# Latent attention: one batch of value matmuls per head, row maxima placed around it, outputs sent by SyncE, w_o's loads reordered

## The chip, the cores and the metric

The kernel runs on one core of a Trainium2 chip, as one launch. The metric is device time in microseconds. A core has TensorE (PE for its matmuls, PEld for its weight loads), VectorE (DVE), ScalarE (ACT), GpSimd (POOL) and SyncE (SP, which only issues transfers here). ACT can issue transfers too; in the profile these rows are called ACTq, those of SP SPq.

## What is computed

Two layers of a decoder over 1024 positions, width 1024, all in float32. Layer 0 is a latent attention with 12 heads, layer 1 a sliding-window attention; each has cross-attention heads on a memory and is followed by an MLP. The change touches the causal attention of layer 0 alone:

```python
def causal_dense_attention(q, k, v):
    b, s, h, dk = q.shape                  # 1, 1024, 12, 96
    nb = s // Q_BLOCK                      # blocks of 128
    scale = dk ** -0.5
    ...
        sc = jnp.einsum('bqhd,bkhd->bhqk', q_blk, k,
                        preferred_element_type=jnp.float32) * scale
        mask = k_idx[None, :] <= t_idx[:, None]
        sc = jnp.where(mask[None, None], sc, NEG)
        p = jax.nn.softmax(sc, axis=-1).astype(v.dtype)
        return jnp.einsum('bhqk,bkhd->bqhd', p, v)
...
    x = x + jnp.concatenate([mix, cross], axis=-1) @ w_o[i]
```

## The kernel before, in words

**Blocks.** A head's scores are computed transposed, keys on the partitions. A block (G, k) has 128 keys (k from 0 to 7) against the 512 queries of half G, from the diagonal on; twelve blocks cover the causal triangle. `scores` (tile pss) makes a block with three matmuls over 97 rows: high part by high part, and the two mixed products of high and low part. Rows 0 to 63 are the plain part of the key, 64 to 95 the rotary part, and row 96 carries the negated row maximum of each query, so that the exponential needs no bias. On diagonal blocks a mask is added, by a fourth matmul in heads 0, 1, 9, 10 and 11 (`mask_by_pe`), by DVE in the others (L1096). ACT takes the exponential into a tile p (L1098), and POOL adds the p of a half up into acc (L1112). Score tiles, pso, psd, psxt and the small psx come from six psum buffers (`ps1`).

**Row maxima.** `row_max(h, i)` makes the scores of query block i of head h from the high parts alone (psx_i, L909, 128 queries by (i+1)*128 keys), and DVE reduces them to a column of m8 (L911, two instructions, the second reads the result out). Those of i above 3 use one psum tile of two banks with a single buffer (`psx`), so psx_7, psx_6, psx_5 and psx_4 follow one another through it. `max_row(h)` transposes m8 (psxt, L890); ACT copies it to mh (L895) and sends it to row 96 of qh by a transfer on its own queue (L896). The table `WHEN` says at which slot of the stream each row maximum of head h stands, counted from the first slot of head h-1; (8, 7) is `max_row`.

**Values.** `values` multiplies p by v (tile pso, L1064, weights of 64 columns) for a batch of blocks. The list `cuts` sets where batches begin: two per head, after six blocks each. `evac(h)` copies pso to `on` (L1143) and sends it out by two transfers (L1145, L1146); `sums(h)` multiplies acc by ones (psd, weights of 32 columns), copies to sm (L1160) and sends it to den (L1163).

**The division.** For groups of heads (0 to 5, 6 to 9, 10) `rc_split` takes reciprocals of den (L1193), sends them to memory (rcd, L1194), `rc_mul` brings them back spread over 64 partitions (rb, L1186, two buffers) and DVE multiplies the outputs by them (L1206). Head 11 is divided apart.

**w_o.** `wq.step()` takes one step of the list load 0, load 1, split 0, load 2, split 1, load 3, split 2, nothing, split 3: a load is 512 KB by SP (wor, L809, two buffers), a split is one ACT and one DVE instruction (woq, L99 and L100).

**Order.** The loop over n, one step per block, writes everything in one stream; `queued()` holds PE to the order written, and `tc.issue_after` places a step behind a named instruction. Where other engines and queues have freedom, the scheduler sets their order when the program is built. Each engine and each queue then takes its instructions strictly in that order.

Of the kernel before, what the change touches and what calls it, by code (L numbers as in the profile page):

```python
# [9 lines left out]
F32 = mybir.dt.float32  # L10
# [9 lines left out]
P = 128  # L20
D = 1024
S = 1024
NT = S // P
KT = D // P
FF = 4096
H = 12
# [29 lines left out]
def trunk(  # L56
# [7 lines left out]
    nc = tc.nc  # L64
    x = x[0]
    out = out[0]
# [26 lines left out]
    def f32(ap):  # L93
        return ap.bitcast(F32)
# [602 lines left out]
    halves = [slice(0, 512), slice(512, 1024)]  # L697
# [176 lines left out]
    def head_tiles(h, lo):  # L874
        r, e = slice((h % 2) * 64, (h % 2) * 64 + 64), slice((h % 4) * 32, (h % 4) * 32 + 32)
        r_, e_ = slice(h * 64, h * 64 + 64), slice(h * 32, h * 32 + 32)
        qh, ql, kh, kl = bufs_[h % 3]
        for t, n, rope in ((kl, kn_d[r_, :], krl_d), (ql, qn_d[r_, :], qr_d[e_, :])) if lo else ((kh, kn[h // 2][r, :], krh_d), (qh, qn[h // 2][r, :], qr[h // 4][e, :])):
            nc.sync.dma_start(out=f32(t[0:64]), in_=n)
            if h < 3 or t is qh or t is ql:  # L880
                nc.sync.dma_start(out=f32(t[64:96]), in_=rope)
        if h in (1, 2) and lo:
            head_ones(h)
# [57 lines left out]
    for e in range(2):  # L941
        c = slice(e * 512, e * 512 + 512)
# [95 lines left out]
    at = pool("at", "right")  # L1038
# [18 lines left out]
    probs, po_, sp_, acc_, first_p, masked, last_mm = {}, {}, {}, {}, {}, [], []  # L1057
# [34 lines left out]
    def probabilities(h, G, k, ps):  # L1092

        c0 = col0(G, k)
        if k >= 4 * G and not mask_by_pe(h, G, k):
            nc.vector.tensor_tensor(ps[:, 0:P], ps[:, 0:P], dmaskT, ALU.add)  # L1096
        p = at.tile([P, 512], F32, tag="p", bufs=14, name=f"p{h}_{G}_{k}")
        masked[0:1] = [nc.scalar.activation(p[:, c0:], ps, AF.Exp, scale=SC).ins]  # L1098
        probs[(h, G, k)] = p
        if (h, "acc") not in acc_:  # L1100
            acc_[(h, "acc")] = at.tile([P, 1024], F32, tag="acc", bufs=2, name=f"acc{h}")
        a = acc_[(h, "acc")][:, G * 512 : G * 512 + 512]
        if (h, G) not in first_p:
            first_p[(h, G)] = p
            return
        q = first_p[(h, G)]
        if q is not None:
            first_p[(h, G)] = None
            if c0:
                nc.scalar.activation(a[:, :c0], q[:, :c0], AF.Copy)  # L1110
        eng = nc.vector if h == H - 1 and G and k in (1, 2, 3, 7) else nc.gpsimd
        eng.tensor_tensor(a[:, c0:], p[:, c0:], (a if q is None else q)[:, c0:], ALU.add)  # L1112
# [25 lines left out]
    def evac(h):  # L1138

        po, _ = po_.pop(h)  # L1140
        r = slice((h % 2) * 64, (h % 2) * 64 + 64)
        on = at.tile([P, 512], F32, tag="on", bufs=2, name=f"on{h}")
        nc.scalar.activation(on, po, AF.Copy)  # L1143
        dst = qn[h // 2][r, :]
        nc.scalar.dma_start(out=dst.rearrange("p (a c) -> p a c", c=256)[:, 0:4:3, :], in_=on[0:64].rearrange("p (a c) -> p a c", c=256))  # L1145
        nc.scalar.dma_start(out=dst[:, 256:768], in_=on[64:128])  # L1146

    def sums(h, G=None):

        acc = acc_[(h, "acc")]  # L1150
        sp = ps1(f"psd{h}_{G}")
        if G is not None:
            sp_[G] = sp
            for g, a, b in quarters(G):
                product(sp[g * 64 : g * 64 + 64, 0:256], ones, acc[:, G * 512 + a : G * 512 + b], start=True, stop=True)
            return
        for i in range(4):
            product(sp[i * 32 : i * 32 + 32, 0:256], ones[:, 0:32], acc[:, i * 256 : i * 256 + 256], start=True, stop=True)
        sm = at.tile([97, 256], F32, tag="sm", bufs=2, name=f"sm{h}")
        nc.scalar.activation(sm, sp[0:97, 0:256], AF.Copy)  # L1160
        c = [c for c in range(3) if h >= GRP[c]][-1]
        d0 = (h - GRP[c]) * NT
        nc.scalar.dma_start(out=den[c][d0 : d0 + NT, :], in_=sm[0:97:32, :])  # L1163

    def last_o(G, tmp, js=range(2)):

# [11 lines left out]
    den = [at.tile([(b - a) * NT, P], F32, name=f"den{a}") for a, b in zip(GRP, GRP[1:])]  # L1178
    rc_d = [dram.tile([b - a, S], F32, name=f"rcd{a}") for a, b in zip(GRP, GRP[1:])]
    r_tiles = {}  # L1180

    def rc_pair(c, j, i):

        rb = at.tile([P, 512], F32, tag="rb", bufs=2, name=f"rb{c}_{j}_{i}")
        for e in range(min(2, GRP[c + 1] - GRP[c] - 2 * j)):
            nc.sync.dma_start(out=rb[e * 64 : e * 64 + 64, :], in_=rc_d[c][2 * j + e, halves[i]].partition_broadcast(64))  # L1186
        return rb

    def rc_split(c):
# [7 lines left out]
    def rc_mul(c):  # L1197
# [15 lines left out]
    NB = len(blocks)  # L1213
    seq = [(h,) + b for h in range(H) for b in blocks_of(h)]

    WHEN = {
        1: ((4, 0), (3, 1), (2, 2), (1, 3), (0, 4), (8, 7)),
        2: ((7, -4), (6, -1), (5, 1), (4, 2), (3, 3), (2, 3), (1, 4), (0, 5), (8, 7)),
        3: ((7, -5), (6, -4), (5, -1), (4, 1), (3, 1), (2, 2), (1, 3), (0, 4), (8, 7)),
    }  # L1220
    ahead = {}
    for h in range(1, H):
# [1 line left out]
            ahead.setdefault((h - 1) * NB + d, []).append((h, i))  # L1224
    muls = iter(())
    waiting = []
    cuts = [*range(0, (H - 1) * NB, 6), *range((H - 1) * NB, len(seq) + 1, 4)]
    batches = {b + 1: (a, b) for a, b in zip(cuts, cuts[1:])}
    for n in range(len(seq) + 2):
        if n < len(seq):  # L1230
            waiting.append(seq[n])
            if n == len(seq) - 1 or seq[n][2] - 4 * seq[n][1] < 3 or seq[n + 1][2] - 4 * seq[n + 1][1] >= 0:
                scores(*waiting[::-1])
                waiting.clear()
        for g, i in ahead.get(n, ()):
            with queued():
                last_mm[0:1] = [row_max(g, i) if i < NT else max_row(g)[-1]]
        if n in batches:
            values(seq[slice(*batches[n])])
            h, j = divmod(n, NB)  # L1240
            if j == 1 and h < H:
                evac(h - 1)
            if h and j == (7 if h < H - 1 else 5):
                sums(h - 1)
            if n == len(seq) - 3:
                sums(H - 1, 1)
                last_o(1, at.tile([P, 256], F32, tag="on", bufs=2, name="rq1"))
        h, j = divmod(n, NB)
        if n < len(seq):
            if j < 2 and h + 2 < H:  # L1250
                head_tiles(h + 2, j)
        if n % 3 == 1 or n > 11 * NB:
            next(muls, None)
        if n >= 9 * NB and n % 3 == 0:
            with tc.issue_after(masked[0]):
                wq.step()
        for c, (a, b) in enumerate(((9 * NB, 9 * NB + 4), (11 * NB + 1, 11 * NB + 4), (11 * NB + 9, 11 * NB + 10))):
            if n == a:
                rc_split(c)
            if n == b:  # L1260
                muls = rc_mul(c)
# [1115 lines left out]
```

## Time and profile before

| | us |
|---|---|
| runs of the kernel (median, lowest to highest) | 2067.89 (2067.59 to 2069.08) |
| the profiled execution | 2066.95 |
| its span, first to last instruction | 2065.2 |
| PE busy | 2048.0 |
| DVE, ACT, POOL busy | 1420.1, 1070.1, 249.4 |
| the twelve heads | about 232 to 410 of the span |

The span leaves 1.75 us around it. PE is called busy from a matmul's start to its modelled end, so small losses between matmuls show as starts that lie further apart, not as idle time; PEld's idle time before a weight load tells what held a matmul up.

### The profile page before, as it was taken

What the parts mean: (1) busy time and instruction counts of PE and PEld (TensorE: products, weight loads), DVE (VectorE), ACT (ScalarE), POOL (GpSimd) and SP (SyncE); (2) the same over time, 40 slices, a digit from 0 to 9 for tenths busy, and PEclk for the clock granted to TensorE, in tenths of its full rate; (3) what the DMA queues carried; (4) which work ended last, traced back from release to release, by engine and by line L of the source; (5) the groups of instructions that cost most, each with busy time, mean ns of one, the idle gap of its engine ahead of it and who ended that gap; (6) DMA issues with size and microseconds to landing.
All of it is one profiled execution on the core that took longest, in us unless ns stands there. A gap on an engine that the chain in (4) does not pass through costs nothing.

```text
span 2065.2 us, 29537 instructions
## 1 busy us (share of the span) xinstructions
PE 2048.0 (99%) x10035; PEld 1677.5 (81%) x10035; DVE 1420.1 (69%) x2817; ACT 1070.1 (52%) x2335; POOL 249.4 (12%) x357
## 2 busy tenths in 40 slices
PE   9999999999999999999999999999999999999998
PEld 7888877688888888888888888778888888888887
DVE  8767556558877777956566625767977777976565
ACT  7564344557545544444445525866744554444453
POOL 1002366500000000000010134510000000000000
PEclk9999999999999999999999999999999999999999
DMA  6213655442544548835442644442444456944442
GB/s 235 90 39 110 189 124 122 134 150 83 178 137 159 163 155 285 293 97 173 137 129 87 148 105 135 109 148 73 162 154 136 160 163 236 327 130 154 122 123 87
DMA packets 190492, 306.83 MB, mean 149 GB/s; under 512 B 18496, under 2 KB 75013, under 8 KB 190341
## 3 DMA queue, kind: packets, MB, share of 16 engines
q1 hardware_dynamic: 182080, 286.20, 44.2%
q0 software_dynamic: 4144, 13.14, 1.8%
q10 hardware_dynamic: 4116, 5.61, 1.0%
q8 instruction: 79, 1.29, 0.3%
q14 instruction: 73, 0.59, 0.1%
HBM read 194.48 MB, written 89.57 MB: 138 GB/s over the span
## 4 chain that ended last, share of the span: by engine, by line
PE 96%; DVE 2%; DMA 1%; ACT 1%; issue 0%; SPq 0%; ACTq 0%; DVEq 0%
PE psu L1612 6%; PE psu L1613 6%; PE psu L1611 6%; PE psy L1949 6%; PE psy L1951 6%; PE psy L1950 6%; PE psz L1949 4%; PE psz L1951 4%; PE psz L1950 4%; PE psv L1612 4%; PE psv L1613 4%; PE psv L1611 4%; PE pss L1064 3%; PE pswo L111 3%; PE pswo L109 3%; PE pswo L110 3%
## 5 line engine op out<-in xcount | busy, mean ns | idle before, releaser
L99 ACT ACTIVATE g<-i 128x512 fp32r<-128x512 f32 x79 | 49.9, 631 | 105.1 <-PE psy L1950 51.0
L1949 PE MATMUL psy<-g 128*128 128x512 f32 x256 | 100.0, 391 | 0.0
L1950 PE MATMUL psy<-g 128*128 128x512 f32 x256 | 99.7, 389 | 0.0
L1951 PE MATMUL psy<-g 128*128 128x512 f32 x256 | 99.7, 389 | 0.0
L911 DVE CUSTOM_DVE_ANT_0 psx<-psx,wide 128x1024 f32<-128x1024 f32 (+7 forms) x96 | 72.7, 766 | 29.1 <-PE psx L909 28.3
L1098 ACT ACTIVATE p<-pss 128x512 f32<-128x512 f32 (+2 forms) x144 | 64.8, 490 | 49.1 <-DVE pss L1096 20.4
L100 DVE TENSOR_TENSOR g<-i,g 128x512 fp32r<-128x512 f32 x79 | 55.5, 703 | 49.5 <-ACT g L99 49.4
L1112 POOL TENSOR_TENSOR acc<-p,acc 128x512 f32<-128x512 f32 (+2 forms) x92 | 86.1, 942 | 13.3 <-ACT p L1098 9.4
L99 ACT ACTIVATE uh<-i 128x512 fp32r<-128x512 f32 x66 | 41.6, 631 | 85.0 <-PE psz L1950 38.8
L99 ACT ACTIVATE i<-mr 128x512 fp32r<-128x512 f32 x78 | 47.8, 628 | 72.4 <-PE psy L1950 23.5
L100 DVE TENSOR_TENSOR uh<-i,uh 128x512 fp32r<-128x512 f32 x66 | 45.5, 690 | 46.6 <-ACT uh L99 46.6
L1949 PE MATMUL psz<-g 128*128 128x512 f32 x192 | 74.7, 389 | 0.0
L1950 PE MATMUL psz<-g 128*128 128x512 f32 x192 | 74.7, 389 | 0.0
L1951 PE MATMUL psz<-g 128*128 128x512 f32 x192 | 74.7, 389 | 0.0
L1510 ACT ACTIVATE mr<-mr,gcol 128x256 f32<-128x256 f32 (+1 forms) x160 | 63.9, 476 | 12.6 <-DMA mr<-in_mlp_w_up_dram 12.6
L100 DVE TENSOR_TENSOR i<-mr,i 128x512 fp32r<-128x512 f32 x78 | 53.5, 687 | 22.8 <-ACT i L99 22.6
L2069 POOL TENSOR_TENSOR wsr<-wsr,gcol 128x1024 f32<-128x1024 f32 x12 | 23.1, 1925 | 343.3 <-ACT i L99 275.0
L1831 DVE TENSOR_TENSOR mqq<-mqf,mqq 128x512 f32<-128x512 f32 x64 | 43.1, 686 | 23.5 <-DMA mqf<-in_mlp_w_down_dram 23.5
L1951 PEld LDWEIGHTS psy<-g 128*128 128x128 f32 x256 | 48.1, 188 | 10.1
L1950 PEld LDWEIGHTS psy<-g 128*128 128x128 f32 x256 | 48.1, 188 | 9.8
L1949 PEld LDWEIGHTS psy<-g 128*128 128x128 f32 x256 | 48.1, 188 | 9.8
L1064 PE MATMUL pso<-p,v 128*64 128x256 f32 (+1 forms) x480 | 53.8, 367 | 0.0
(659 smaller groups left out, 6746.3 us busy)
## 6 DMA issues: line engine op xcount, KB each, us to landing
i<-hd SPq DMA_DIRECT2D x154, 256.0 KB
hd<-uh SPq DMA_DIRECT2D x76, 256.0 KB
hd<-ul SPq DMA_DIRECT2D x76, 256.0 KB
mr<-in_mlp_w_up_dram SPq DMA_DIRECT2D x36, 512.0 KB
hd<-x SPq DMA_DIRECT2D x72, 256.0 KB
mr<-hd SPq DMA_DIRECT2D x70, 256.0 KB
d<-in_mlp_w_up_dram SPq DMA_DIRECT2D x32, 512.0 KB
mqf<-in_mlp_w_down_dram SPq DMA_DIRECT2D x32, 512.0 KB
```

The lines of the kernel that those rows point to most:

```text
L99: a = nc.scalar.activation(hi, src, AF.Copy)
L100: d = nc.vector.tensor_tensor(lo, src, f32(hi), ALU.subtract)
L911: nc.vector.tensor_tensor_reduce(ps[:, :n], ps[:, :n], wide[h > 1][:, S - n :], -1.0, 3.0e38, ALU.add, ALU.min, accum_out=m)
L1064: last_mm[0:1] = [nc.tensor.matmul(*args, skip_group_check=True, **kw).ins]
L1098: masked[0:1] = [nc.scalar.activation(p[:, c0:], ps, AF.Exp, scale=SC).ins]
L1112: eng.tensor_tensor(a[:, c0:], p[:, c0:], (a if q is None else q)[:, c0:], ALU.add)
L1611: nc.tensor.matmul(ps, wh[:, k, :], xh[:, k, :], start=p in (1, 2, 5) and k == 0, stop=False, skip_group_check=True)
L1612: nc.tensor.matmul(ps, wh[:, k, :], xl[:, k, :], start=False, stop=False, skip_group_check=True)
L1613: nc.tensor.matmul(ps, wl[:, k, :], xh[:, k, :], start=False, stop=k == 3, skip_group_check=True)
L1949: nc.tensor.matmul(ps, ah[:, j, :], bh, start=start, stop=False, skip_group_check=True)
L1950: nc.tensor.matmul(ps, ah[:, j, :], bl, start=False, stop=False, skip_group_check=True)
L1951: nc.tensor.matmul(ps, al[:, j, :], bh, start=False, stop=k == NP - 1, skip_group_check=True)
```

## The change

1. `cuts`: head 0 keeps two batches of six blocks; the twelve blocks of each of heads 1 to 10 form one batch, at slot 1 of the next head; head 11 stays as it was.
2. `sums(h-1)` stands at slot 1 of head h for every head, right behind the batch and `evac`, where it stood at slot 7 (5 in the last head).
3. The tile p has 16 buffers instead of 14.
4. The three output transfers of a head (two of `on`, one of den) are issued by SP, not by ACT.
5. `WHEN`: psx_7 now stands before the blocks (1, 2) and (0, 3), `max_row` behind them; some others are a slot later or earlier.
6. Both halves of `head_tiles(h + 2)` are issued at slot 0 (before at slots 0 and 1).
7. w_o's steps: every second slot from n = 116 (before every third from 108), and also behind the last rb transfer written so far (`last_rb`).

```diff
--- before.py
+++ after.py
@@ -1094,7 +1094,7 @@
         c0 = col0(G, k)
         if k >= 4 * G and not mask_by_pe(h, G, k):
             nc.vector.tensor_tensor(ps[:, 0:P], ps[:, 0:P], dmaskT, ALU.add)
-        p = at.tile([P, 512], F32, tag="p", bufs=14, name=f"p{h}_{G}_{k}")
+        p = at.tile([P, 512], F32, tag="p", bufs=16, name=f"p{h}_{G}_{k}")
         masked[0:1] = [nc.scalar.activation(p[:, c0:], ps, AF.Exp, scale=SC).ins]
         probs[(h, G, k)] = p
         if (h, "acc") not in acc_:
@@ -1142,8 +1142,8 @@
         on = at.tile([P, 512], F32, tag="on", bufs=2, name=f"on{h}")
         nc.scalar.activation(on, po, AF.Copy)
         dst = qn[h // 2][r, :]
-        nc.scalar.dma_start(out=dst.rearrange("p (a c) -> p a c", c=256)[:, 0:4:3, :], in_=on[0:64].rearrange("p (a c) -> p a c", c=256))
-        nc.scalar.dma_start(out=dst[:, 256:768], in_=on[64:128])
+        nc.sync.dma_start(out=dst.rearrange("p (a c) -> p a c", c=256)[:, 0:4:3, :], in_=on[0:64].rearrange("p (a c) -> p a c", c=256))
+        nc.sync.dma_start(out=dst[:, 256:768], in_=on[64:128])
 
     def sums(h, G=None):
 
@@ -1160,7 +1160,7 @@
         nc.scalar.activation(sm, sp[0:97, 0:256], AF.Copy)
         c = [c for c in range(3) if h >= GRP[c]][-1]
         d0 = (h - GRP[c]) * NT
-        nc.scalar.dma_start(out=den[c][d0 : d0 + NT, :], in_=sm[0:97:32, :])
+        nc.sync.dma_start(out=den[c][d0 : d0 + NT, :], in_=sm[0:97:32, :])
 
     def last_o(G, tmp, js=range(2)):
 
@@ -1179,11 +1179,13 @@
     rc_d = [dram.tile([b - a, S], F32, name=f"rcd{a}") for a, b in zip(GRP, GRP[1:])]
     r_tiles = {}
 
+    last_rb = []
+
     def rc_pair(c, j, i):
 
         rb = at.tile([P, 512], F32, tag="rb", bufs=2, name=f"rb{c}_{j}_{i}")
         for e in range(min(2, GRP[c + 1] - GRP[c] - 2 * j)):
-            nc.sync.dma_start(out=rb[e * 64 : e * 64 + 64, :], in_=rc_d[c][2 * j + e, halves[i]].partition_broadcast(64))
+            last_rb[0:1] = [nc.sync.dma_start(out=rb[e * 64 : e * 64 + 64, :], in_=rc_d[c][2 * j + e, halves[i]].partition_broadcast(64)).ins]
         return rb
 
     def rc_split(c):
@@ -1215,8 +1217,8 @@
 
     WHEN = {
         1: ((4, 0), (3, 1), (2, 2), (1, 3), (0, 4), (8, 7)),
-        2: ((7, -4), (6, -1), (5, 1), (4, 2), (3, 3), (2, 3), (1, 4), (0, 5), (8, 7)),
-        3: ((7, -5), (6, -4), (5, -1), (4, 1), (3, 1), (2, 2), (1, 3), (0, 4), (8, 7)),
+        2: ((7, -4), (6, -1), (5, 0), (4, 1), (3, 1), (2, 3), (1, 4), (0, 5), (8, 7)),
+        3: ((7, -6), (6, -4), (5, -1), (4, 1), (3, 1), (2, 3), (1, 4), (0, 5), (8, 7)),
     }
     ahead = {}
     for h in range(1, H):
@@ -1224,7 +1226,7 @@
             ahead.setdefault((h - 1) * NB + d, []).append((h, i))
     muls = iter(())
     waiting = []
-    cuts = [*range(0, (H - 1) * NB, 6), *range((H - 1) * NB, len(seq) + 1, 4)]
+    cuts = [0, 6, *range(NB, (H - 1) * NB, NB), *range((H - 1) * NB, len(seq) + 1, 4)]
     batches = {b + 1: (a, b) for a, b in zip(cuts, cuts[1:])}
     for n in range(len(seq) + 2):
         if n < len(seq):
@@ -1240,19 +1242,20 @@
             h, j = divmod(n, NB)
             if j == 1 and h < H:
                 evac(h - 1)
-            if h and j == (7 if h < H - 1 else 5):
+            if 0 < h < H and j == 1:
                 sums(h - 1)
             if n == len(seq) - 3:
                 sums(H - 1, 1)
                 last_o(1, at.tile([P, 256], F32, tag="on", bufs=2, name="rq1"))
         h, j = divmod(n, NB)
         if n < len(seq):
-            if j < 2 and h + 2 < H:
-                head_tiles(h + 2, j)
+            if j == 0 and h + 2 < H:
+                head_tiles(h + 2, 0)
+                head_tiles(h + 2, 1)
         if n % 3 == 1 or n > 11 * NB:
             next(muls, None)
-        if n >= 9 * NB and n % 3 == 0:
-            with tc.issue_after(masked[0]):
+        if n > 9 * NB + 7 and n % 2 == 0:
+            with tc.issue_after(masked[0]), tc.issue_after(last_rb[0]):
                 wq.step()
         for c, (a, b) in enumerate(((9 * NB, 9 * NB + 4), (11 * NB + 1, 11 * NB + 4), (11 * NB + 9, 11 * NB + 10))):
             if n == a:
```

Three places show the order. The first is PE at the end of head 4 (psx6 are the row maxima of head 6, psxt5 the transposed maxima of head 5); before:

```order
L1064 MATMUL pss4_1_2_3300<-ckh_549,ckl_550 128x512 x2
L1064 MATMUL pss4_0_3_3303<-ckh_549,ckl_550 128x128 x2
L1064 MATMUL pss4_1_2_3300<-ckh_549,ckl_550 128x512
L1064 MATMUL pss4_0_3_3303<-ckh_549,ckl_550 128x128
L890 MATMUL psxt5_3315<-ident_63,m8_5_3155 8x128
L909 MATMUL psx6_7_3321<-kh0_2218,qh0_2216 128x512 x2
L1064 MATMUL pso4_1_3325<-p4_1_0_3224,v_1462 64x256 x2
...
L1064 MATMUL pso4_1_3325<-p4_1_5_3287,v_1462 64x128
L1064 MATMUL psd3_None_3338<-acc3_3061,ones_2563 32x256 x4
L1064 MATMUL pss4_0_2_3346<-ckh_549,ckl_550 128x256 x3
L909 MATMUL psx6_6_3354<-kh0_2218,qh0_2216 128x512
L909 MATMUL psx6_6_3354<-kh0_2218,qh0_2216 128x384
```

and now:

```order
L909 MATMUL psx6_7_3309<-kh0_2218,qh0_2216 128x512 x2
L1064 MATMUL pss4_1_2_3313<-ckh_549,ckl_550 128x512 x2
L1064 MATMUL pss4_0_3_3316<-ckh_549,ckl_550 128x128 x2
L1064 MATMUL pss4_1_2_3313<-ckh_549,ckl_550 128x512
L1064 MATMUL pss4_0_3_3316<-ckh_549,ckl_550 128x128
L890 MATMUL psxt5_3328<-ident_63,m8_5_3143 8x128
L1064 MATMUL pss4_0_2_3333<-ckh_549,ckl_550 128x256 x3
L909 MATMUL psx6_6_3341<-kh0_2218,qh0_2216 128x512
L909 MATMUL psx6_6_3341<-kh0_2218,qh0_2216 128x384
```

The batch and the sums between psx6_7 and psx6_6 are gone; psx6_7 has moved ahead of (1, 2) and (0, 3), so that these, psxt5 and (0, 2) are all that lies between psx6_7 and psx6_6.

The second is PE at the start of head 5, where the whole batch of head 4 now stands, cut after its first rows:

```order
L909 MATMUL psx6_4_3392<-kh0_2218,qh0_2216 128x320 x2
L909 MATMUL psx6_3_3396<-kh0_2218,qh0_2216 128x512
L1064 MATMUL pso4_1_3399<-p4_1_0_3211,v_1462 64x256 x2
L1064 MATMUL pso4_1_3399<-p4_0_0_3225,v_1462 64x256 x2
L1064 MATMUL pso4_1_3399<-p4_1_4_3272,v_1462 64x256 x2
```

It goes on to the blocks up to (1, 7) and (0, 3), 20 instructions in all (16 of 256 columns, 4 of 128), and then the four matmuls of psd4. Before, psd of a head stood six blocks after its last values.

The third is SP in head 9; before:

```order
L1186 DMA rb0_2_1_4308<-rcd0_2572 64x512
...
L881 DMA ql2_2555<-qrd_1944 32x1024
L809 DMA wor0_0_1_4112<-in_w_o_dram 128x2x512
L809 DMA wor0_0_2_4207<-in_w_o_dram 128x2x512
L1186 DMA rb0_2_1_4308<-rcd0_2572 64x512
L1186 DMA rb0_2_0_4363<-rcd0_2572 64x512 x2
L809 DMA wor0_0_3_4294<-in_w_o_dram 128x2x512
```

and now:

```order
L1145 DMA fa1_100<-on8_4083 64x2x256
L1146 DMA fa1_100<-on8_4083 64x512
L1163 DMA den6_2570<-sm8_4092 8x1x128
L809 DMA wor0_0_1_4193<-in_w_o_dram 128x2x512
L1188 DMA rb0_2_1_4309<-rcd0_2572 64x512 x2
L1188 DMA rb0_2_0_4347<-rcd0_2572 64x512 x2
L809 DMA wor0_0_2_4283<-in_w_o_dram 128x2x512
```

The load wor0_0_2, which reuses the buffer of wor0_0_0 and so waits for its split, stood ahead of the second half of rb0_2_1; it now stands behind all four halves, and wor0_0_1 stands between den of head 8 and rb0_2_1.

## Rows read from the trace of the kernel before

**Rows 1.** The page, part 1: busy time and its share of the span.
```profile
PE 2048.0 (99%) x10035; PEld 1677.5 (81%) x10035; DVE 1420.1 (69%) x2817; ACT 1070.1 (52%) x2335; POOL 249.4 (12%) x357
```

**Rows 2.** Windows from one head's first score to the next (heads 4, 7, 8, 10): us, busy (instructions) by engine, clock.
```profile
288.03:302.13 14.10, 14.10 (x100) 10.49 (x98) 8.18 (x25) 6.66 (x17) 9.39 (x10) 1.00 0.50 112
...
330.35:345.05 14.70, 14.38 (x99) 10.49 (x98) 8.96 (x26) 6.66 (x17) 9.38 (x10) 1.00 0.58 147
345.05:359.96 14.91, 14.46 (x99) 10.48 (x98) 10.50 (x29) 6.72 (x17) 10.22 (x10) 1.00 0.63 145
...
374.91:392.94 18.03, 15.46 (x102) 11.46 (x100) 7.92 (x16) 8.27 (x18) 9.90 (x10) 0.91 0.28 82
```

**Rows 3.** Timeline of head 4, PE and PEld: start, us, operation, count, idle before and releaser.
```profile
290.04 1.73 PE L1064 MATMUL pso<-p,v 128*64 128x256 f32 x16
...
291.70 0.96 PE L1064 MATMUL pss<-ckh,ckl 97*128 97x512 f32 x3
...
292.50 0.34 PE L909 MATMUL psx<-kh,qh 96*128 96x384 f32 x1
...
295.63 0.27 PE L890 MATMUL psxt<-ident,m 128*8 128x128 f32 x1
...
295.66 0.71 PE L909 MATMUL psx<-kh,qh 96*128 96x512 f32 x2
...
296.30 2.60 PE L1064 MATMUL pso<-p,v 128*64 128x256 f32 x24
...
298.82 0.64 PE L1064 MATMUL psd_None<-acc,ones 128*32 128x256 f32 x8
...
299.39 0.62 PE L1064 MATMUL pss<-ckh,ckl 97*128 97x256 f32 x3
...
301.67 0.30 PEld L909 LDWEIGHTS psx<-kh,qh 96*128 96x128 f32 x2 [0.17 <-DVE m L911]
...
302.13 0.40 PE L1064 MATMUL pss<-qh,kh 97*128 97x512 f32 x1
...
302.36 0.40 PE L1064 MATMUL pss<-ql,kh 97*128 97x512 f32 x1
```

**Rows 4.** The same stretch, DVE's read-out of psx_7 and ACT's issue of mh.
```profile
296.40 1.23 DVE L911 CUSTOM_DVE_ANT_0 psx<-psx,wide 128x1024 f32<-128x1024 f32 x1 [0.28 <-PE psx L909]
...
296.54 0.71 ACTq L896 DMA_DIRECT2D qh<-mh  x1
...
297.55 0.14 DVE L911 DVE_READ_ACCUMULATOR2_ANT m<- 128x1 f32 x1
```

**Rows 5.** Timeline of head 10, DVE and PE around the multiplications by rb.
```profile
374.17 0.14 DVE L911 DVE_READ_ACCUMULATOR2_ANT m<- 128x1 f32 x1
...
376.13 0.45 PE L1064 MATMUL pss<-ckh,ckl 97*128 97x512 f32 x1
...
376.51 1.65 DVE L1206 TENSOR_TENSOR qn<-rb,qn 128x512 f32<-128x512 f32 x2 [2.20 <-DMA rb<-rcd]
...
379.15 0.80 PE L909 MATMUL psx<-kh,qh 96*128 96x320 f32 x3 [2.57 <-DVE m L911]
...
379.88 2.49 PE L1064 MATMUL pso<-p,v 128*64 128x256 f32 x16
...
383.96 0.41 PE L909 MATMUL psx<-kh,qh 96*128 96x384 f32 x1
```

**Rows 6.** The chain that ends last in 360 to 412 us: start, us, what.
```profile
368.95 2.03 DVE woq L100
371.00 0.39 SPq L809
...
371.43 4.99 DMA rb<-rcd
...
391.44 1.70 DMA den<-sm
...
396.04 3.04 DMA rb<-rcd
```

## What the change does to the time, forecast blind

> **What bounds the kernel now.** I read the page's first part: TensorE is busy 2048.0 of 2065.2 us [rows 1]. So whatever is gained must come out of TensorE's own instruction stream or out of the few places where it waits. The change stays inside the twelve heads of layer 0, so the table of windows came next, one window per head [rows 2]. A steady head takes 14.10 us with PE busy for all 14.10, DVE 8.18, ACT 6.66 and POOL 9.39: four engines of which only PE is full. Heads 7 and 8 take 14.70 and 14.91, and head 10 takes 18.03 with 15.46 busy at a mean granted clock of 0.91. Third, the timeline of one steady head [rows 3, 4], to see where PE's stream is thinner than its matmuls need; fourth, the timeline of head 10 [rows 5]; last, the chain that ends the stretch around it [rows 6]. The profiled execution took 2066.95 us, 0.94 below the median of the runs, 2067.89; I make the sum against 2066.95 and put the 0.94 back at the end. A measurement of this kernel tells about 0.2%, 4.1 us, from no change.
>
> **Part 1, one batch of values for two.** In a head, PE goes from scores to values and back twice. The 16 records at 290.04 last until the scores at 291.70, 1.66 us; the 24 at 296.30 last until the sums at 298.82, 2.52 us [rows 3]. Of the 24, four have 128 columns, of the 16 also four; counting those as half, 22 units take 2.52 and 14 take 1.66: 0.1075 per unit and 0.155 that does not depend on the size. After the batch three score matmuls of 512 columns take 0.80 (291.70 to 292.50) where a matmul takes 0.23 (302.13 to 302.36), so 0.11 is lost there. Ahead of the batch the row-max pair that starts at 295.66 needs 0.64 to the first value matmul, the same sort of pair at 301.67 only 0.46 to 302.13; part of the 0.18 belongs to the transposition just before, so I take 0.10, near the loss on the way out. Together 0.36 us for one way in and out. Ten heads lose one such pair: **-3.6** (bounds -3.1, with no loss on the way in, and -4.4, with 0.18). The sums keep their place behind a batch and their price; the moved evacuation follows the batch as before.
>
> **Part 2, the row maxima.** psx_7 and psx_6 share one psum tile, so psx_6 waits until DVE has read psx_7. Before, the batch of values lay between them and hid it. psx_7 starts at 295.66 and DVE's read-out of it ends at 297.55 + 0.14 [rows 3, 4]: 2.03 us. Now PE has in that time the pair itself (0.46), three matmuls of 512 columns (0.69), three of 128 and the transposition (about 0.12 each, 0.48), three of 256 (0.35): 1.98. It comes 0.05 too early, and a weight load that could not run ahead costs 0.17, as the idle time of PEld before psx_5 shows at 301.67. About 0.24 us in each of the seven heads whose diagonal is masked by DVE (2 to 8); in heads 9 and 10 the mask is a matmul, two of them lie there, and PE comes later than DVE. **+1.7** (bounds 0, if DVE starts sooner than it did, and 3.5, if the mask of block (0,3) pushes it out by its 0.3 as well).
>
> **Part 3, w_o's loads and the stall in head 10.** DVE stood 2.20 us waiting for the broadcast rb, then did two multiplications (1.65) ahead of psx_5 [rows 5]. PE's last matmul before was at 376.13 and would have been followed at 376.36; psx_4 came at 379.15: 2.79 us lost. Then the clock fell: from 379.88 to 383.96 PE did what takes 290.04 to 292.50 elsewhere, 4.08 for 2.46 plus one mask matmul of 0.11, so 1.5 more at the lower of its two levels (1.2 for 2.4 GHz). Together 4.3. Its cause is in the chain [rows 6]: the w_o load at 371.00 waited for DVE's split at 368.95, and the second half of rb stood behind it on SP's queue and took 4.99 us to land. After the change that load stands behind all of rb's transfers; only one w_o load that waits for no split is ahead of them, and it follows den of head 8. That den is sent about 7.5 us into head 9 (two score blocks, 40 value records of 4.4, the sums and their copy), so near 367.5 to 368 on the old scale. rb issued at 368.5 with the same 4.99 lands at 373.5; DVE asks for it when psx_6 is done, at 374.3. The wait is then gone, and one multiplication of 0.82 ahead of psx_5 instead of two is covered. **-4.3** (bounds: -1.0, if rb is still 2 us late and only the second multiplication moves out of the way; -4.3).
>
> **Part 4, outputs by SP.** Three issues per head leave ACT's queue, each near the 0.71 of the issue that stays [rows 4]; ACT is busy 6.66 of 14.10 and no PE matmul waits for it in a steady head, so the saving hides: 0. What is queued behind them on SP: the next heads' tiles stand ahead of them, so only w_o's loads and rb come later. The Trainium skill (DMA: Bandwidth & Descriptors, Issuing engines are not separate DMA queues) says that another issuing engine saves only the issuing time; by it too this term is 0. The two extra p buffers and head_tiles in one slot are 0: the row maxima that need those tiles lie near the end of the head.
>
> **Part 5, the row of maxima.** After psxt, ACT copies it and sends it into row 96 of qh; the next head's first score needs it. Before, psxt stood at 295.63 and the head at 302.13, 6.50 us later, with values and sums (296.30 to 299.39, 3.09) and the psx_7 pair (0.64) between. These go ahead of psxt or behind the head's start: 2.77 are left, less 0.11 for the slow first score, plus 0.24 from part 2: 2.90. ACT's issue is 0.91 after psxt [rows 4], so the transfer must land within 1.9 to 2.0 us. The trace before has no wait for it; its nearest rows are the small den at 1.70, in time, and above it rb at 3.04 and 4.99 among loads [rows 6]. I take in time for quiet heads, and 0.5 us late in the three heads whose end now lies among w_o or rb loads (7, 9, 10): **+1.5** (bounds 0 and 3 x 1.1 by the 3.04). In the first heads the row maxima of head 2 are closer together: **+0.3** (0 to 1).
>
> Sum: -3.6 + 1.7 - 4.3 + 1.5 + 0.3 = **-4.4**: 2066.95 becomes 2062.55, and with the 0.94 **2063.5**.
>
> **Rivals.** *A, all of it is gained.* psx_6 is in time, the row of maxima lands everywhere, and the 0.6 and 0.8 by which heads 7 and 8 exceed 14.10 go with the reordered loads: -3.6 - 4.3 - 1.4 + 0.3 = -9.0, 2058.9. For it: the deficit of part 2 is only 0.05, and 1.70 is under 1.9. Against: a late weight load costs its 0.17 even when the deficit is small. *B, slower: the row of maxima is late in every head.* The price is the landing less 1.9, ten times. By rb's 3.04 that is +11; with -3.6 + 1.7 - 4.3 = -6.2 the kernel gets slower by 4.9: 2072.8. It decides from a landing of 2.5 us on (ten times 0.6 undoes the -6.2). A clock that falls after such waits, as in head 10, would add to it. Against: the issue comes when the head's loads have long been done, as den's does. The Trainium skill (DMA: Bandwidth & Descriptors, Queues, rings and completion order) says that each DMA engine alternates between queues packet by packet, so that ACT's small transfer is not stuck behind SP's loads but shares with them; no row before shows the two together. *C, a stall in head 10 stays.* rb still lands behind a w_o load, only another one: part 3 is -1.0 and the sum -1.1, 2066.8. For it: the load and rb are still neighbours on SP. Against: they no longer wait for a split. *D, the order does not change what PE does:* the psx chain on DVE takes back the 0.36 of every head; with part 3 at half, -2.2 + 1.8, near 2067.5. Against: DVE is busy 8.18 of 14.10.
>
> **How the numbers follow.** Forecast 0.50, its own range 2061 to 2066, with over half of it under 2063.75 (faster by 0.2%); A 0.20, C 0.14, D 0.07, B 0.09. Faster: 0.29 + 0.20 = 0.49; slower: two thirds of B and a little of the rest, 0.07; the same 0.44. The range leaves out the lower half of A and B but for its mild end: 2059.5 to 2070.0.
>
> **What would show it.** Right: heads 3 to 6 take about 13.98 (14.10 - 0.36 + 0.24); PEld shows one wait for issue before pso in a head, not two, and a new wait before psx_6 for DVE's read-out; DVE's multiplication has no wait for rb, and head 10's clock stays at 1.00. Wrong: PE waits at a head's first score for the DMA of mh (B), or DVE still waits for rb (C); steady heads of 13.74 would be A.

## The result, and the profile after

The changed kernel takes 2080.0 us (median of 6 runs, 2072.82 to 2081.01) against 2068.44 (6 runs, 2067.47 to 2069.14). The ratio is 1.005, interval 1.004 to 1.0061: slower by 11.6 us, where 2063.5 was forecast and the range ended at 2070.0. The profiled execution took 2079.93, its span grew from 2065.2 to 2078.2. The page's first lines:

```profile
span 2078.2 us, 29539 instructions
...
PE 2053.9 (99%) x10035; PEld 1683.2 (81%) x10035; DVE 1424.7 (69%) x2817; ACT 1072.2 (52%) x2335; POOL 253.1 (12%) x357
```

PE is busy only 6 us longer than in [rows 1], while the span is 13 us longer. The table cuts the span at the first score of heads 0, 1, 7 and 11 and at the ninth matmul of pswo (behind the last wait there), from the starts in the timelines:

| us | head 0 | heads 1 to 6 | 7 to 10 | head 11 to w_o | from there to the last matmul |
|---|---|---|---|---|---|
| before | 12.56 | 85.82 | 62.58 | 19.00 | 1646.10 |
| after | 19.24 | 84.45 | 64.44 | 26.39 | 1645.11 |

About 2.6 us of value work (the 24 records) has moved from heads 1 to 6 into head 11, since each batch now runs in the next head; like for like, heads 1 to 6 are 1.2 us slower and the end 4.8. Windows of the changed kernel, one head each (heads 0, 4, 7, 8, 10; columns as in [rows 2]):

```profile
231.90:251.14 19.24, 17.39 (x82) 13.60 (x80) 5.89 (x15) 6.32 (x14) 8.31 (x11) 0.73 0.47 138
...
292.96:306.93 13.97, 13.97 (x99) 10.64 (x98) 8.29 (x25) 6.86 (x17) 9.36 (x11) 1.00 0.49 114
...
335.59:352.72 17.13, 14.13 (x99) 10.56 (x98) 11.19 (x28) 7.79 (x19) 12.15 (x14) 0.99 0.72 184
352.72:369.72 17.00, 17.00 (x98) 12.51 (x98) 7.29 (x23) 6.05 (x14) 7.14 (x8) 0.81 0.35 94
...
385.96:400.03 14.07, 13.51 (x100) 10.64 (x100) 8.67 (x17) 8.28 (x16) 9.83 (x8) 1.00 0.22 60
```

The steady head 4 takes 13.97 instead of 14.10, and head 10 takes 14.07 at full clock instead of 18.03 at 0.91. But head 0 runs at a mean clock of 0.73, and heads 7 and 8 take 34.1 us together, head 8 at 0.81. What PE waited for there (total, times, longest):

```profile
PE pss L1064 <- DMA qh<-mh: 3.7, 3, 3.0
PE psd L1064 <- DVE acc L1112: 1.8, 1, 1.8
PE pss L1064 <- POOL maskr L1045: 1.7, 1, 1.7
```

None of these three waits is in the trace of before. The one for mh, the row of maxima, stands at the first scores of heads 8 (3.00), 11 (0.56) and 6 (0.16); head 10 has one of 0.71 besides, under the name ckh. **The first** is in head 0:

```profile
234.94 0.16 POOL L1042 MEMSET ones<- 128x64 f32 x1 [23.78 <-DMA qnd<-lo]
...
235.28 0.30 POOL L1045 CAST maskr<-dmaskT 128x128 fp32r<-128x128 f32 x1
...
235.63 0.33 PE L1064 MATMUL pss<-maskr,identr 128*128 128x128 f32 x1 [1.72 <-POOL maskr L1045]
...
236.41 0.63 PE L1064 MATMUL pss<-qh,kh 97*128 97x512 f32 x1
...
236.84 0.63 PE L1064 MATMUL pss<-ql,kh 97*128 97x512 f32 x1
```

The memset of ones waits for the transfers that send out the low parts (lo), then come the casts, and the mask matmul of the first diagonal block waits 1.72 us for maskr. The next scores start 0.43 apart, not 0.23: the lower level of the clock. **The steady head**, 4:

```profile
302.42 0.75 PE L909 MATMUL psx<-kh,qh 96*128 96x128 f32 x3
...
304.36 0.14 DVE L911 DVE_READ_ACCUMULATOR2_ANT m<- 128x1 f32 x1
...
304.55 0.30 PEld L909 LDWEIGHTS psx<-kh,qh 96*128 96x128 f32 x2
304.56 0.67 PE L909 MATMUL psx<-kh,qh 96*128 96x512 f32 x2
...
304.90 0.63 ACTq L896 DMA_DIRECT2D qh<-mh  x1
...
306.93 0.40 PE L1064 MATMUL pss<-qh,kh 97*128 97x512 f32 x1
```

From psx_7's start (second of the three at 302.42, so 302.48) to the end of the read-out at 304.50 it is 2.02, and psx_6's weight load starts only 0.01 before its matmul: it could not run ahead. The row of maxima is issued at 304.90 and the next head starts at 306.93 with no wait. **The second wait**, head 7:

```profile
342.37 0.65 SPq L1145 DMA_DIRECT2D qn<-on  x1
...
344.41 2.40 SPq L1188 DMA_DIRECT2D rb<-rcd  x4
...
346.86 0.59 SPq L809 DMA_DIRECT2D wor<-in_w_o_dram  x1
...
347.51 0.63 ACTq L896 DMA_DIRECT2D qh<-mh  x1
...
352.72 0.77 PE L1064 MATMUL pss<-qh,kh 97*128 97x512 f32 x1 [3.00 <-DMA qh<-mh]
```

SP sends head 6's outputs at 342.37, behind them the four halves of rb0_0 at 344.41, then w_o's 512 KB at 346.86. The 4 KB of mh, issued at 347.51, let PE go on at 352.72, 5.2 us later. rb0_0 thus leaves 8.8 us into head 7. Before, it left at 337.77, 7.4 us into the head: most of the 6.6 us between the two times is head 0's loss, which moves all of head 7. **The third** is at the end, SP, DVE and PE (three fences):

```profile
406.19 4.19 SPq L1188 DMA_DIRECT2D rb<-rcd  x4
...
411.77 0.60 SPq L1163 DMA_DIRECT2D den<-sm  x1
```

```profile
413.26 0.69 DVE L1208 TENSOR_TENSOR fa<-rb,fa 128x512 f32<-128x512 f32 x1 [2.58 <-DMA rb<-rcd]
413.87 1.08 DVE L1112 TENSOR_TENSOR acc<-p,acc 128x512 f32<-128x512 f32 x2
...
419.98 1.08 DVE L1208 TENSOR_TENSOR fa<-rb,fa 64x512 f32<-64x512 f32 x1 [2.22 <-DMA rb<-rcd]
```

```profile
417.90 0.65 PE L1064 MATMUL psd<-acc,ones 128*64 128x256 f32 x4 [1.79 <-DVE acc L1112]
...
425.39 0.50 PE L111 MATMUL pswo<-woq,x 128*128 128x512 f32 x1 [2.19 <-DVE x L100]
```

DVE waits 2.58 us for the last halves of rb1, and behind that multiplication stand the adds of head 11 for which psd waits 1.79. In the kernel before, DVE had these adds ahead of its last two multiplications by rb1, and the wait for rb (0.47) behind them:

```profile
401.25 1.09 DVE L1112 TENSOR_TENSOR acc<-p,acc 128x512 f32<-128x512 f32 x2 [0.62 <-POOL acc L1112]
...
403.00 1.49 DVE L1112 TENSOR_TENSOR acc<-p,acc 128x512 f32<-128x512 f32 x2
...
404.97 0.69 DVE L1206 TENSOR_TENSOR fa<-rb,fa 128x512 f32<-128x512 f32 x1 [0.47 <-DMA rb<-rcd]
```

Counted from head 11's start, rb1's last half does not leave later than before (9.8 us into the head, before 10.5). It is the order on DVE that now lets it hold up the adds. den10 leaves 11.7 us into the head (before 8.8), and rb2, which depends on it, now stands ahead of the last reciprocals (before, behind them): pswo waits 2.19.

### The profile page after: what moved, and what is told of

Its sections match the earlier page's. It is cut to its first block, busy times and chain, and to the rows that moved or that the text cites. A ratio compares the mean times of both kernels' runs of the same rounds, so it can differ in the third digit from the quotient of the medians.

```text
span 2078.2 us, 29539 instructions
## 1 busy us (share of the span) xinstructions
PE 2053.9 (99%) x10035; PEld 1683.2 (81%) x10035; DVE 1424.7 (69%) x2817; ACT 1072.2 (52%) x2335; POOL 253.1 (12%) x357
## 4 chain that ended last, share of the span: by engine, by line
PE 95%; DVE 2%; DMA 1%; issue 1%; ACT 1%; SPq 0%; POOL 0%; DVEq 0%; POOLq 0%; ACTq 0%
PE psu L1614 6%; PE psu L1616 6%; PE psu L1615 6%; PE psy L1954 6%; PE psy L1953 6%; PE psy L1952 6%; PE psz L1952 4%; PE psz L1954 4%; PE psz L1953 4%; PE psv L1616 4%; PE psv L1614 4%; PE psv L1615 4%; PE pss L1064 3%; PE pswo L111 3%; PE pswo L109 3%; PE pswo L110 3%
## 5 line engine op out<-in xcount | busy, mean ns | idle before, releaser
L1112 POOL TENSOR_TENSOR acc<-p,acc 128x512 f32<-128x512 f32 (+2 forms) x92 | 88.3, 969 | 11.6 <-ACT p L1098 7.2
L1513 ACT ACTIVATE d<-d,gcol 128x256 f32<-128x256 f32 x128 | 53.5, 497 | 0.0
```

The costliest lines, as they stand in the source:

```text
L1513: nc.scalar.activation(w[:, k, :], w[:, k, :], AF.Copy, scale=g_mlp[layer][:, k0 + k : k0 + k + 1])
```

## Experiments

The theory after the result (theory A in the expectations) puts the loss outside the batch itself: **addresses** (two more p buffers move ones, identr and maskr onto space that is still being sent from) and **the outputs on SP's queue**, which make rb0_0 and den10 late and so heads 7, 8 and the end. Its rivals: the new order as such, and w_o's reordering.

### e1: before, with 16 p buffers

```diff
-        p = at.tile([P, 512], F32, tag="p", bufs=14, ...
+        p = at.tile([P, 512], F32, tag="p", bufs=16, ...
```

> The kernel before with one edit: the tile p has 16 buffers, not 14. The order on every engine is that of before; only addresses move. Theory A (addresses: the pool grows by 4 KB, the small constants ones, identr and maskr move onto the space of the outgoing low parts, and their memset and casts wait for those transfers): POOL's memset of ones starts at about 234.9 us, not 231.6, PE waits about 1.7 us for maskr in head 0, the clock falls there, and the kernel is 4 to 6 us slower than before, about 2073. Rival B (more p buffers are harmless, the head-0 wait of the changed kernel comes from its new order): within 1 us of before, 2068.

2070.15 us, ratio 1.0014 (1.0005 to 1.0023): slower, by 2.0 in the median, less than the 4 to 6 of theory A. The built program's list of waits names the cause; POOL's memset before and with 16 buffers:

```
L1042 MEMSET ones_2563 128x64 [waits PE_49]
L1042 MEMSET ones_2563 128x64 [waits DMAHW4_49,DMAHW5_49,DMAHW2_49,DMAHW6_49,DMAHW1_49,DMAHW7_49,DMAHW0_49,DVE_49]
```

Seven transfer queues and DVE have come in; the order of PE's matmuls is the same. POOL in the timeline, and the window of head 0:

```profile
234.66 0.16 POOL L1042 MEMSET ones<- 128x64 f32 x1 [23.53 <-DVE m L911]
```

```profile
231.85:250.84 18.99, 17.40 (x81) 13.60 (x80) 5.89 (x15) 6.30 (x14) 8.31 (x11) 0.73 0.49 139
```

The line names DVE as what came last. POOL in fact stood until 234.41 in the wait for two of the transfer queues, on one of which the low parts sent at 231.53 landed at 234.38, and passed everything else within 0.25 us. The memset starts 3 us late, and head 0 takes 18.99, near the 19.24 of the changed kernel. Not every run pays alike: six of ten lie at 2068.97 to 2070.74 with a mean clock of 0.998 or 0.999, four at 2072.63 to 2074.83 with 0.996 or 0.997, the profiled one (2074.13) among them. By these groups the wait costs 1 to 2 us, and some 4 to 5 more where the clock falls behind it.

### e2: the changed kernel, constants at their old addresses

```diff
+    at.tile([P, 512], F32, tag="rb", bufs=2, name="rbx")
     ones = at.tile([P, 64], F32, name="ones")
```

> The changed kernel with one edit: the space of rb is taken in the pool ahead of ones, identr and maskr, so that these lie where they lay before; p keeps 16 buffers and the order on every engine is that of the changed kernel. Theory A (addresses): the memset of ones is back at about 231.6, head 0 takes about 12.6 us instead of 19.24, and the kernel is 4 to 6 us faster than the changed one, about 2074 to 2075. Rival B (order): no change, 2080.

2073.63 us, ratio to before 1.002 (1.0008 to 1.0032); 6.4 less than the changed kernel, a little more than theory A said. Head 0 takes 12.55. What is left in heads 7 and 8, and PE's wait between them (4.6 of it at head 8):

```profile
PE pss L1064 <- DMA qh<-mh: 5.6, 3, 4.6
```

```profile
329.26:348.02 18.76, 14.13 (x100) 10.57 (x98) 11.20 (x28) 7.77 (x19) 13.64 (x15) 0.95 0.73 178
348.02:364.35 16.33, 16.33 (x98) 12.20 (x98) 7.29 (x23) 6.04 (x14) 5.59 (x7) 0.85 0.33 87
```

The runs of e2 fall into two groups: four at 2067.34 to 2069.70, six at 2073.32 to 2077.05, the profiled one (2073.93) among these.

### e3 and e5: outputs back on ACT

e3 replaced the issuing engine by its text and so also moved four other kinds of transfers to ACT (the low parts, the loads of x and two in the MLP); e5 moves the three alone, and keeps e2's addresses.

```diff
-        nc.sync.dma_start(out=dst.rearrange(...
-        nc.sync.dma_start(out=dst[:, 256:768], ...
-        nc.sync.dma_start(out=den[c][d0 : d0 + NT, :], ...
+        nc.scalar.dma_start(out=dst.rearrange(...
+        nc.scalar.dma_start(out=dst[:, 256:768], ...
+        nc.scalar.dma_start(out=den[c][d0 : d0 + NT, :], ...
```

> The changed kernel with the three output transfers of a head back on ACT's queue. Theory A (on SP the outputs stand ahead of rb and rb ahead of them, so rb0_0 is sent 6.6 us later and collides with w_o's load and mh in head 7, and den of head 10 is sent behind rb1_1): PE's 3.0 us wait for mh at the start of head 8 is gone, den10 is sent before 405, the stretch from head 11's start to the first w_o matmuls is back near 18 us from 25, and the kernel is 8 to 12 us faster than the changed one, 2068 to 2072. Rival B (w_o's reordering makes both): within 2 us of the changed kernel.

> The changed kernel with two things undone: ones, identr and maskr lie where they lay before, and the three output transfers of a head are on ACT's queue. Theory A (addresses and SP's queue make the loss up to head 11, POOL's late sums the rest): head 0 12.55 us, heads 7 to 10 together 59 to 60 (62.58 before, 64.4 in the changed kernel), from head 11's start to the first w_o matmul still 21 to 22 (16.46 before, of which 2.6 is value work that moved there), in all 2067 to 2069.5. Rival B (the w_o order makes the late end and the waits for mh): heads 7 to 10 stay over 63, in all 2072 or more.

e3: 2072.25 us; heads 7 to 10 59.26 instead of 64.44, the wait at head 8 gone, as theory A said, but from head 11 to w_o still 24.3 (26.39 in the changed kernel, 19.00 before): the outputs' queue makes at most 2.1 us of the late end, so that part of the theory falls. e5: 2067.57, ratio 1.0 (0.9991 to 1.001): no change against before. Windows of e5, heads 0, 7, 8, 10:

```profile
231.69:244.25 12.56, 12.45 (x82) 10.18 (x81) 5.89 (x15) 6.33 (x14) 7.91 (x10) 1.00 0.72 210
...
328.34:343.08 14.74, 14.04 (x99) 10.63 (x98) 9.36 (x25) 6.66 (x17) 9.56 (x10) 1.00 0.71 183
343.08:358.07 14.99, 14.31 (x99) 10.65 (x98) 10.37 (x29) 6.71 (x17) 10.27 (x11) 1.00 0.61 160
...
373.23:388.33 15.10, 13.73 (x101) 10.50 (x100) 8.07 (x16) 8.73 (x19) 10.45 (x10) 1.00 0.23 57
```

Heads 7 to 10 take 59.99, at full clock. rb0_0 leaves 3.4 us into head 7, where it left 8.8 us into it in e2, and no head from 1 to 10 waits for mh (head 11 does, 1.35 us). Since e5 differs from e2 in the outputs' queue alone, that queue cost 6.1 us by the medians, and about 4 by the ratios to before (1.002 and 1.0), since e2's median lies between its two groups. The end is nearly as long as in e2 (25.74 to the ninth w_o matmul, 26.25 there), longer than expected (23.79 to the first one, where 21 to 22 was said), and a wait in it is unchanged:

```profile
403.20 1.73 PE L1064 MATMUL pso<-p,v 128*64 128x256 f32 x14
406.75 0.65 PE L1064 MATMUL psd<-acc,ones 128*64 128x256 f32 x4 [1.82 <-DVE acc L1112]
```

### e4 and e6: w_o's steps as before

```diff
-        if n > 9 * NB + 7 and n % 2 == 0:
-            with tc.issue_after(masked[0]), tc.issue_after(last_rb[0]):
+        if n >= 9 * NB and n % 3 == 0:
+            with tc.issue_after(masked[0]):
```

> The changed kernel with w_o's steps as before (every third slot from n = 108, behind masked alone), outputs on SP. Theory A (SP's outputs): rb0_0 is still sent at about 344.4, but no w_o load stands among the transfers at the end of head 7, so the wait for mh there is shorter, about 1 to 2 us; den10 still behind rb1_1, the tail still about 25 us; 2 to 5 us faster than the changed kernel, 2075 to 2078. Rival B (w_o's reordering): both waits gone, 8 to 12 us faster, 2068 to 2072.

> As the run before it, and w_o's steps as before the change as well; left of the change are the batch of twelve, the sums behind it, the row maxima, p's 16 buffers and the tiles in one slot. Theory P1 (the splits, now later, run on DVE beside POOL's adds and make both longer, so sums of heads 10 and 11 are late): the end gets 2 us shorter than in the run before it, 19.5, and the whole 2065 to 2067. Theory P2 (the batch alone makes POOL late, since a head's first adds start behind it): the end stays at 21 to 22 and PE still waits for acc ahead of psd in head 11; the whole 2067 to 2070.

e4 (on the changed kernel): 2072.95, 7.0 less, between what the two theories said. The wait of 3.0 us for mh at head 8 is gone, with rb0_0 sent as late into head 7 as ever (8.8 us) but no w_o load beside it; So the halves of rb0_0 alone do not make it. Whether the load alone would, no run shows: in e5, where the wait is gone too, the load also leaves earlier (6.9 us into head 7, mh at 12.6). The end stays (26.15). e6 (on e5): 2070.96; the end 25.89 against 25.74. P1 falls: the later splits do not set it. P2 had the end stay, but at 21 to 22 to the first w_o matmul, where it takes 23.94.

### e7: before, with the new w_o steps

The edit of e4 reversed, on the kernel before.

> The kernel before with w_o's steps as in the changed one and nothing else. If the 4.3 us stall of head 10 came from the w_o load ahead of rb, heads 7 to 10 take 58.3 instead of 62.58 and the clock stays up there. Rival: later splits and loads delay the end, rb of the second group and the last sums, by 2 to 5 us, so that the whole is 2066 to 2069 in spite of it. Without that: 2064.

2066.32 us, ratio 0.9993 (0.9984 to 1.0003). Head 10:

```profile
374.40:388.96 14.56, 13.88 (x101) 10.50 (x100) 8.08 (x16) 8.03 (x18) 9.69 (x9) 1.00 0.33 92
```

It takes 14.56 at full clock instead of 18.03 at 0.91 [rows 2], heads 7 to 10 58.78 instead of 62.58. But from head 11 to w_o it is 23.74, at a mean clock of 0.86, instead of 19.00 at full clock: psd of head 11 waits 2.0 us for DVE's adds; the rival had named a late end of 2 to 5 us. So the reordering alone gives back at the end what it gains in head 10.

### e8: adds of head 10 by DVE

```diff
-        eng = nc.vector if h == H - 1 and G and k in (1, 2, 3, 7) else nc.gpsimd
+        eng = nc.vector if h == H - 1 and G and k in (1, 2, 3, 7) or h == H - 2 and k in (3, 6, 7) else nc.gpsimd
```

> The second of these four (batch of twelve, outputs on ACT, old w_o steps, old addresses) with the adds of head 10's blocks k = 3, 6, 7 of acc done by DVE instead of POOL. If POOL's lag sets the end, PE's wait ahead of psd of head 10 (about 1.5 us) and of head 11 (about 2 us) shrinks and the end gets 1.5 to 3 us shorter than there. If DVE itself is late by then (splits, multiplications and reciprocals in front), nothing is gained or the end is up to 2 us longer.

2070.63 us, and the end 28.25 against 25.89 in e6: psd of head 11 now waits 4.1 us for DVE, while the wait of psd of head 10 for POOL (0.8 in e6) is gone. POOL's lag is not what sets the end there; DVE's queue is.

### e9 and e10: w_o's second half behind the last rb

The order on SP showed why DVE waits for rb1: wor0_1_0, the first load of w_o's second half, waits for a split and stands between rcd6 and rb1. The edit puts these loads behind rb:

```diff
-                        w1.step()
+                        with tc.issue_after(last_rb[0]) if layer == 0 else ExitStack():
+                            w1.step()
```

> Batch of twelve, outputs on ACT, old w_o steps, old addresses (e6), and the loads of w_o's second half issued behind the last rb transfer, so that wor0_1_0, which waits for a split, no longer stands between rcd6 and rb1 on SP. Theory A (the late end is a queue matter: rb1 late, so DVE's multiplications are late, and the adds of head 11 queue behind them): PE's wait of 1.85 us ahead of psd of head 11 and the low clock after it go, head 11's start to the first w_o matmul 20 us instead of 23.9, the whole 2064 to 2067. Rival P2 (POOL is late because of the batch): PE still waits ahead of psd of head 10 or 11, 23 us or more, the whole 2069 to 2071.

> The same edit on the kernel with the new w_o steps (e5). wor0_0_3, which waits for a split behind rc1, still stands ahead of rb1, so by theory A about half of the gain: head 11's start to the first w_o matmul 21.5 to 22.5 instead of 23.8, the whole 2065 to 2067. Rival P2: no change, 2067.5.

e9 (on e6): 2067.18, 3.8 less; e10 (on e5): 2067.38, 0.2 less, no change. In e9 the wait ahead of psd of head 11 is gone, and the end takes 23.79 at full clock instead of 25.89 at 0.93. (The profiled execution of e6, 2068.25, is one of its two shortest, so the traces show less of the gain than the medians.) What is left there, of the longer waits:

```profile
PE pss L1064 <- ACT p L1098: 1.0, 1, 1.0
PE psd_None L1064 <- POOL acc L1112: 0.9, 2, 0.7
```

psd of head 10 (psd_None) waits for POOL: with the whole batch behind a head's first two blocks, POOL's first adds come later in the head (8.7 us into head 4, before 6.5). Both theories hold a part: the load ahead of rb1 is worth 2.1 us with the clock, and waits of 0.9 for POOL are left. In e10 the end is 24.92: wor0_0_3 is still ahead of rb1, and psd still waits 0.9 for DVE.

### e11 and e12: the same edit without the batch

> The kernel before with the new w_o steps (e7) and w_o's second half behind the last rb; values in two batches, outputs on ACT, 14 buffers. Theory A: heads 7 to 10 stay at 58.8 and the end, 21.55 there, goes back to 17 to 18: 2061.5 to 2064, the fastest of all. Rival (the splits themselves make the end late, whatever the queue): end 20 or more, 2065 to 2067.

> The kernel before with only w_o's second half behind the last rb; w_o's first half stays as it was, so wor0_0_2 is still ahead of rb0_2. Heads 7 to 10 stay at 62.5 with the 4.3 us of head 10; the end, which has rb in time before, changes by less than 1 us: 2066.5 to 2068.5, no change.

e11 (e7 with that edit: before, the new w_o steps, w_o's second half behind rb): 2065.16 us, 2064.71 to 2065.51, ratio 0.9986 (0.9977 to 0.9995), 2.6 us faster than the kernel before and the fastest of all here. Head 10, and head 11 up to w_o:

```profile
374.68:389.26 14.58, 13.89 (x101) 10.49 (x100) 8.10 (x16) 8.04 (x18) 9.72 (x9) 1.00 0.34 91
389.26:410.06 20.80, 19.09 (x126) 13.17 (x126) 15.55 (x22) 11.88 (x30) 10.78 (x11) 1.00 0.37 108
```

Both at full clock: the gain in head 10 is kept and the end takes 20.80 (17.83 to the first w_o matmul, within the 17 to 18 of theory A). The time stayed above the 2064 expected; psd still waits 0.9 us for DVE. e12 (that edit on the kernel before; in it the old w_o steps too are placed behind the last rb written so far, and head 10 keeps its 18.03): 2068.18, 1.0001, no change, as expected.

Two pairs differ by the batch and what belongs to it (sums, row maxima, buffers, tiles), with the load behind rb in both. With the new w_o steps the batch costs 2.2 us (e10, 2067.38, against e11, 2065.16), with the old ones it gains 1.0 (e9, 2067.18, against e12, 2068.18). So it has no price of its own: it depends on what stands around it, and in e10 wor0_0_3 still stands just ahead of rb1, which it does not in e11.

## Why the prediction was wrong

*Part 1 and part 2* held. A steady head was to take 13.98 and takes 13.97: the saved way in and out of the values, less the wait of psx_6, both in their places. Two figures of the working are off without moving the forecast by more than 0.2: with no loss on the way in, part 1's bound is 0.155 + 0.11 = 0.265 a head, -2.6 and not -3.1, and part 2's 0.05 and 0.17 make 0.22, not 0.24. That this sum is only 0.13 a head was in the forecast; heads 1 to 6 as a whole lose 1.2 all the same, most of it in head 1 (13.91, where 15.29 less the 2.6 and the switch makes 12.3), where psx waits 0.6 and 0.3 us for DVE. The term "+0.3 (0 to 1)" for it was 1.3 too small.

*Part 3* held for the stretch that it looked at: 4.3 was forecast, e7 shows 3.8 in heads 7 to 10. But e7 also shows 4.7 lost from head 11 to w_o (23.74 against 19.00), for which part 3 had nothing. Of its signs one was missed without a price: DVE still waits 1.0 us for rb at 385.50, and PE does not wait for that.

*Part 4* is the step that failed, twice. "The two extra p buffers and head_tiles in one slot are 0": I looked at how many buffers there are and not at where a pool that is 4 KB larger puts the rest. It costs 2.0 us by itself in the median (e1) and 6.4 in the changed kernel, with the clock (after against e2). And "only w_o's loads and rb come later. ... 0": I named what is queued behind the outputs and did not follow it. With the outputs ahead of it rb0_0 leaves 8.8 us into head 7, with them on ACT's queue 3.4 (e2 and e5), and so it and w_o's load stand just ahead of mh, which has 2 us to land. e5 against e2: 6.1 us by the medians. (The 6.6 us in the expectation of e3 is counted from the start of the span, and 5.2 of it is the later start of head 7.) The two undos together take off 12.4 us (2080.0 to 2067.57), the whole loss against the kernel before.

*Part 5* had the mechanism, the right margin (quiet heads have 2.03 and wait for nothing) and the right three heads: the waits behind heads 7, 9 and 10 are 3.00, 0.71 and 0.56, where 0.5 each was forecast. Mis-sized is the first, and with it the bound "3 x 1.1 by the 3.04": in head 7 the 4 KB took 5.2 us, and the lower clock in head 8 followed the wait. I had taken rb's 3.04 for the bound and passed over the 4.99 in the same group [rows 6], the transfer just behind a w_o load: less the 2.0 of margin it gives 3.0. The trace of before also holds a row with ACT's small transfer and SP's loads together, which rival B says it does not: mh of head 7 is issued at 339.46 among rb0_0's halves, and by the counts of landed packets it landed at 343.8, 4.4 us later (1.8 in quiet heads), hidden by a margin of 5.6. The Trainium skill (DMA: Bandwidth & Descriptors, Queues, rings and completion order), which I read as speaking against a late mh, says that an engine alternates between queues packet by packet. Here the small transfer on ACT's queue took 5.2 us beside SP's loads, and 6.8 in e2, so it gave no protection worth counting on.

*Missing* was any term for the end of head 11. The sum stopped at head 10, as if what follows only waited for PE. There a chain runs from den over rb to DVE's multiplications, and in the changed kernel to the adds of head 11 behind them. Before the change psd waits for nothing there; in the changed kernel, e2 and e4 to e8 it waits 1.6 to 4.1 us for DVE, in e5 to e8 at a mean clock of 0.86 to 0.93 from head 11 to w_o, and e9 shows the wait gone when the load ahead of rb1 is moved. Like for like the end is 4.8 us longer in the changed kernel. Each of two parts of the change is enough for it: w_o's steps alone (e7) make it 4.7 longer, the batch with the old steps (e6) 4.3 when the 2.6 that moved there is taken off.

*Rival B* ended on the right side with its mechanism in four heads and not in ten, over 1 us in one of them, and with causes that it didn't name: the addresses and the queue of the outputs. It was given 0.09.

Shown by an undo: the addresses (e1, e2), the outputs' queue (e5 against e2), the load ahead of rb1 (e9 against e6). Only argued: that the order on DVE is why rb1 holds up psd now and did not before (the two traces show the adds ahead of its last multiplications before and behind them now; no run changed that alone); that POOL's later start in each head is what makes psd of head 10 wait (e9 shows the wait and its releaser; e8 took it away, but what that is worth is hidden by its own wait for DVE). Open: what the batch costs by itself, since the two pairs of runs above disagree.

## What to carry to other kernels

A larger buffer count is a change of addresses: look whether the small tiles allocated behind it now wait for something that they did not wait for (the built program's list of waits shows it before anything runs). When a transfer is moved to another queue, follow what then stands behind it to its own consumer, with that consumer's slack, and look at what that engine has queued behind the wait; an order that frees slack at one place (values between psxt and the next head) takes it from another. Sum up to the point where the next phase starts, not to the last stage that the change edits.

## What the runs showed of the hardware

Nearly the same wait of PE was followed by the lower clock in one execution and not in another. In e1, behind a wait of 1.5 us for maskr, head 0 ran at 0.73; in e4, behind one of 1.4 us in the same place, it went on at full clock, 14.19 us against 18.99:

```profile
232.11:246.30 14.19, 12.67 (x82) 10.05 (x80) 5.89 (x15) 6.32 (x14) 8.28 (x11) 1.00 0.64 186
```

That it differs between executions of one program too is what e1's two groups of times and mean clocks suggest (above); only one of its runs was profiled. So a short wait has two prices, its own and, with some chance, some 5 us more, and kernels with several of them spread: the changed kernel and e2 to e4 span 8 to 10 us from run to run, e11 0.8.

A 4 KB transfer on ACT's queue took 5.2 us up to PE's start, and 6.8 in e2, when SP had issued 1 MB (four halves of rb at 128 KB and a w_o load of 512 KB) in the 3.1 us before it. In e4, behind the four halves alone, PE went on 2.0 us after its issue.
